# A two-layer hybrid decoder trunk on one core: four conditioning loads summed by TensorE behind the output projection, and slot weights read out of the transposed slot matrix

## The chip, the core and the metric

The kernel runs on one core of a Trainium2 chip. The metric is the device time of one execution in microseconds. Before the change it is 1552.6 us (median of 3 runs, 1552.41 to 1552.89).

## The reference, cut to what matters

256 tokens of width 1024 go through two layers in float32. Each layer has a token mixer (a combined input projection, three attention-like branches, per-channel gates, an output projection) and a mixture of experts. Both are conditioned: a vector `c` gives six rows of 1024 values per layer, two shifts, two scales and two gates of the residual.

```
c_act = silu(c)
for l in range(2):
    sh1, sc1, gt1, sh2, sc2, gt2 = split(c_act @ ada_w[l] + ada_b[l], 6)     # ada_w[l]: 1024 x 6144
    h = rms_norm(x, norm1_g[l]) * (1 + sc1) + sh1
    x = x + gt1 * token_mixer(h)                       # ends in merged @ out_w[l]
    h = rms_norm(x, norm2_g[l]) * (1 + sc2) + sh2
    group = argmax(softmax(h @ w_grp)); top 2 of the 8 experts in that group, weights w1, w2
    x = x + gt2 * sum over the token's two experts of weight * (silu(h @ W1[e]) * (h @ W3[e])) @ W2[e]
out = rms_norm(x, final_g)
```

There are 32 experts per layer; each has 6.3 MB of weights, so one layer of experts reads 201 MB from HBM.

## The kernel before, in words

**Loads.** All weights come over one queue (SP) in one order that is fixed when the program is built. A ring of slots of 1 MB receives them; the next load of the plan is issued as soon as its slot is given back, and SP issues strictly in order. The ring has 12 slots and grows for the expert stage: two tiles on the right side before the output projection, parts of the work area `ar`, and three tiles on the left side (`more_left`), which are the space of the split buffers that the mixer no longer needs. At most 8 loads are under way at a time.

**Conditioning ("ada").** `ada_w` is read in loads of 1 MB, 512 columns by half of the 1024 rows, 24 per layer. They are not needed at once, so they are spread behind the mixer's weights in the plan. A load is summed in one of two ways (`ada`, L485). By DVE: four instructions of 128x512 that add weight times `c` into `acc` (L509, L511), then one small matmul per 512 columns that adds up the partitions. Or by PE: four matmuls with the 32 columns of `cz` as stationary operand and the load as moving operand, each in a column strip of its own of the array. The loop `chain` (L1045) runs through the loads: twelve loads for this layer's second norm and first gate, all by DVE; then four loads for the second gate, and in layer 0 eight more for the next layer. It parks itself (`later`, L1039) before the last `ADA_TAIL` loads, and those go to PE: 2 in either layer, after the router's first part has been written.

**Output projection (`out`, L1167).** PE multiplies the merged branches with `out_w`, both split in a high and a low part, so three matmuls for each product. Column half n = 0 ends first, its residual (L588: DVE, DVE, then a square sum on ACT) and its half of the router (`router_half`, L1215: transposes of x, copies by ACT, products with the router's weights) run beside half n = 1. After half n = 1 the other half of the router follows. In ACT's queue the copy of the transposed first 128 tokens stands ahead of the square sum of the second 128.

**Routing (`route`, `choose`).** A chain of short DVE instructions, for the two token tiles alternately, finds group, experts and slots. For the first tile small matmuls without use (`pulse`) follow DVE's steps, to keep PE at work. At the end of the chain PE sums the slot counts (`mb`), DVE makes the first one-hot matrices, and PE gathers the tokens of the first pair of experts.

**Expert stage (`moe`, L1344).** 16 pairs of experts per layer, 64 slots for each expert. Per pair PE does: the first up projection (weights `exp_w1`), `combine` of the pair before (8 matmuls), `slots_of` (L1365), the second up projection (`exp_w3`), the gather of the next pair, four transposes, the down projection (`exp_w2`). `slots_of` makes unweighted one-hot matrices of tokens by slots, transposes them into PSUM, multiplies the untransposed ones with the weights W (two matmuls with 2 moving columns), copies each expert's 64 weights to `wsl` and the transposed matrix to `OT`. `wsl` scales the down projection's result of this pair; `OT` is used by `combine` one pair later.

Of the kernel before, what the change touches and what calls it, by code (L numbers as in the profile page):

```python
# [14 lines left out]
ALU = mybir.AluOpType  # L15
AX = mybir.AxisListType
# [4 lines left out]
NT = 2  # L21
# [3 lines left out]
CAP = 64  # L25
# [20 lines left out]
A_END = 9216  # L46


ADA_TAIL, ADA_FIRST = 2, 2

ADA_BEHIND = {2048: 1, 2560: 1, 0: 1}

# [113 lines left out]
class Trunk:  # L166
# [773 lines left out]
    def run(self, gen):  # L940
        for _ in gen:
            self.step(self.live)
# [84 lines left out]
    def mixer(self, l):  # L1027
        nc, run, finish = self.nc, self.run, self.finish
# [16 lines left out]
        def chain():  # L1045
            self.rowsA = yield from self.ada(l, 4, range(6), space, self.R, range(6))
            yield from self.gs(l, 1, 12 * l + 6, self.rowsA)
            yield from self.router_terms(l)
            while not self.y_free and gr not in self.live:
                yield  # L1050
            yield from self.gate_rows(12 * l + 4, A_GT1, self.rowsA)
            self.gated = True
            yield from later(0)
            self.rowsB = yield from self.ada(l, 10, range(2), lambda i: later(i + 1), self.v(A_RB, 512),
                                             range(min(2, inline // 2)))
            if l + 1 < DEPTH:
                rows = yield from self.ada(l + 1, 0, range(4), lambda i: later(i + 5 if i >= 0 else -1), self.acc[:, 1],
                                           range((inline - 4) // 2))
                yield from self.gs(l + 1, 0, 12 * l + 12, rows)
            self.parked = True  # L1060

        ga = chain()
# [104 lines left out]
        def out():  # L1167
            pa = [[self.bank("g") for _ in range(NT)] for _ in range(2)]
            for h in range(2):
                for n in range(2):  # L1170
                    for j in range(4):
                        wh, wl = self.next_w()
                        m = (self.yr[1], self.hr[0])[h][:, :, j]
                        for t in range(NT):
                            ts = slice(128 * t, 128 * t + 128)
                            self.mm3(pa[n][t], m[:, 0, ts], m[:, 1, ts], wh, wl, h + j == 0, h + j == 4)
                        self.pump()
                        yield
                    if h == 0:
                        continue  # L1180
                    if n:
                        self.finish(half)
                    half = self.router_half(n)
                    for t in range(NT):
                        self.residual(t, n, pa[n][t], self.v(A_RES + 512 * t, 512))
                        self.free(pa[n][t])
                        if n:
                            next(half)
                    if n:
                        self.together(half)  # L1190
                    else:
                        self.live.append(half)
# [6 lines left out]
        while not self.gated:  # L1199
            self.step(self.live)  # L1200
        run(out())
        while not self.parked:
            self.step(self.live)
        pool = self.open_extra(l, "left", 3)
        parts = [pool.tile([P, 2, 512], F32R, name=f"{n}_{l}", tag=n) for n in ("yh", "yl")]
        self.yp = [[p[:, n] for p in parts] for n in range(2)]
        self.ring.grow([self.v(A_MORE[2], 2048)], l)
        self.tail = True
        for _ in range(ADA_FIRST):
            next(ga, None)  # L1210
        self.route()
        self.rest = ga

# [33 lines left out]
    def choose(self, t, r):  # L1247
        nc = self.nc
        one = lambda: self.small(1)
        tt, tsc, red = nc.vector.tensor_tensor, nc.vector.tensor_scalar, nc.vector.tensor_reduce  # L1250
        stt = nc.vector.scalar_tensor_tensor
        rt = self.v(A_RT + 132 * t, 132)
        lg, lm, o1, o2 = rt[:, 0:36], rt[:, 36:68], rt[:, 68:100], rt[:, 100:132]
        stt(lg, self.psr[:, 64 * t:64 * t + 36], r, self.sb, ALU.mult, ALU.add)
        if t == NT - 1:
            self.free(self.psr)
        yield
        gmax, nmax, gsum, m2 = one(), one(), one(), one()
        g4 = lg[:, 0:4]
        c4, off = self.small(4), self.small(4)  # L1260
        red(gmax, g4, AX.X, ALU.max)
        yield
        stt(c4, g4, gmax, self.desc, ALU.is_equal, ALU.mult)
        self.pulse(t, c4)
        yield
        red(m2, c4, AX.X, ALU.max)
        self.pulse(t, m2)
        yield
        tsc(off, self.desc, m2, NEG, ALU.not_equal, ALU.mult)
        self.pulse(t, off)  # L1270
        yield
        tt(lm.rearrange("p (g e) -> p g e", g=4), lg[:, 4:36].rearrange("p (g e) -> p g e", g=4),
           off[:, :, None].to_broadcast([P, 4, 8]), ALU.add)
        yield
        top, idx, fi = self.small(8), self.small(8), self.small(2)
        nc.vector.max(top, lm)
        self.pulse(t, top)
        yield
        nc.vector.max_index(idx.bitcast(U32), top, lm)
        yield  # L1280
        nc.vector.tensor_copy(fi, idx[:, 0:2].bitcast(U32))
        yield
        tsc(o1, self.iota0, fi[:, 0:1], None, ALU.is_equal)
        self.pulse(t, o1)
        yield
        stt(self.mb[:, t], self.iota0, fi[:, 1:2], o1, ALU.is_equal, ALU.add)
        d, e2, den, w1, w2 = (one() for _ in range(5))
        ps = self.bank("s")
        if t == 1:
            self.mm(ps[:, 0:32], self.ones16, self.mb[:, 0], True, False)  # L1290
        self.mm(ps[:, 0:32], self.sU, self.mb[:, t], t == 0, True)
        yield
        tsc(nmax, gmax, -1.0, None, ALU.mult)
        tt(d, top[:, 1:2], top[:, 0:1], ALU.subtract)
        nc.scalar.activation(self.small(4), g4, AF.Exp, bias=nmax, accum_out=gsum)
        nc.scalar.activation(e2, d, AF.Exp)
        yield
        stt(self.rr[:, t], ps[:, 0:32], 1.0, self.mb[:, t], ALU.add, ALU.mult)
        self.free(ps)
        yield  # L1300
        self.one_hot(0, t, r)
        tsc(o2, self.iota0, fi[:, 1:2], None, ALU.is_equal)
        yield
        tsc(den, e2, 1.0, gsum, ALU.add, ALU.mult)
        yield
        nc.vector.reciprocal(w1, den)
        yield
        tt(w2, w1, e2, ALU.mult)
        tsc(self.W[:, t], o1, w1, None, ALU.mult)
        yield  # L1310
        stt(self.W[:, t], o2, w2, self.W[:, t], ALU.mult, ALU.add)
        yield

    def one_hot(self, p, t, by=None):

        oh = self.v(A_OH[t] + 2 * CAP * (p % 2), 2 * CAP)
        for i in range(2):
            e = 2 * p + i
            o, r = oh[:, CAP * i:CAP * i + CAP], self.rr[:, t, e:e + 1]
            if by is None:  # L1320
                self.nc.vector.tensor_scalar(o, self.iota1[:, 0:CAP], r, None, ALU.is_equal)
            else:
                self.nc.vector.tensor_scalar(o, self.iota1[:, 0:CAP], r, by, ALU.is_equal, ALU.mult)  # L1323
        return oh


# [17 lines left out]
    def moe(self, l):  # L1344
        nc, tc = self.nc, self.tc
# [4 lines left out]
        wsl = lambda p: self.wsl[:, p % 2:p % 2 + 1]  # L1350
# [9 lines left out]

        def wanted(p):

            return [self.one_hot(p, t, self.rs[:, t:t + 1]) for t in range(NT)]

        def slots_of(p):  # L1365

            ps = S[2]
            oh = [self.one_hot(p, t) for t in range(NT)]
            for t in range(NT):
                self.tr(ps[:, 128 * t:128 * t + 128], oh[t])  # L1370
            for t in range(NT):
                self.mm(ps[:, 256:258], oh[t], self.W[:, t, 2 * p:2 * p + 2], t == 0, t == 1)
            for e in range(2):
                es = slice(64 * e, 64 * e + 64)
                nc.vector.tensor_copy(wsl(p)[es], ps[es, 256 + e:257 + e])  # L1375
            nc.vector.tensor_copy(self.OT, ps[:, 0:256])

        def combine(p, halves=(0, 1)):

# [16 lines left out]
        for p in range(NE // 2):  # L1396
# [19 lines left out]
            elif p != OVERFLOW:  # L1416
                combine(p - 1)
            nc.scalar.activation(hid, G[0], AF.Silu)  # L1418
            slots_of(p)
            following = iter(()) if end else self.gather(wanted(p + 1), hg[(p + 1) % 2])  # L1420
            up(G[1], "exp_w3")
            nc.vector.tensor_tensor(hid, hid, G[1], ALU.mult)  # L1422
# [13 lines left out]
            ps = G[0]  # L1436
# [4 lines left out]
            for h, n0, nn in self.w2_parts(l, p):  # L1441
                sv = [self.ring.take((l, "exp_w2", 2 * p + e, h, n0)) for e in range(2)]
                for n in range(n0, n0 + nn):
                    for i in range(2):
                        j = 2 * h + i
                        for e in range(2):
                            es = slice(64 * e, 64 * e + 64)
# [193 lines left out]
```

## Time and profile before

| | |
|---|---|
| runs | 1552.6 us median (1552.41 to 1552.89) |
| profiled execution | 1548.41 us, of which the span is 1546.7 us |
| PE / PEld busy | 1471.0 / 901.9 us |
| DVE / ACT busy | 662.7 / 451.4 us |
| load queue (q1) | 532.89 MB, 85.3% of 16 DMA engines' span |
| granted TensorE clock, mean | 0.982 |

PE is TensorE's matmuls, PEld its weight loads, DVE VectorE, ACT ScalarE, SP the queue that issues the loads. [...] A float32 matmul shows as two records, a transpose as one. The two expert stages lie at 335 to 790 us and at 1081 to 1534 us; the two stretches from output projection to the first expert at 296 to 335 us and at 1044 to 1081 us.

### The profile page before, as it was taken

What the parts mean: (1) busy time and instruction counts of PE and PEld (TensorE: products, weight loads), DVE (VectorE), ACT (ScalarE), POOL (GpSimd) and SP (SyncE); (2) the same over time, 40 slices, a digit from 0 to 9 for tenths busy, and PEclk for the clock granted to TensorE, in tenths of its full rate; (3) what the DMA queues carried; (4) which work ended last, traced back from release to release, by engine and by line L of the source; (5) the groups of instructions that cost most, each with busy time, mean ns of one, the idle gap of its engine ahead of it and who ended that gap; (6) DMA issues with size and microseconds to landing.
All of it is one profiled execution on the core that took longest, in us unless ns stands there. A gap on an engine that the chain in (4) does not pass through costs nothing.

```text
span 1546.7 us, 21257 instructions
## 1 busy us (share of the span) xinstructions
PE 1471.0 (95%) x8326; PEld 901.9 (58%) x8326; DVE 662.7 (43%) x1756; ACT 451.4 (29%) x897; POOL 5.9 (0%) x10
## 2 busy tenths in 40 slices
PE   6898899999999999999979989999999999999996
PEld 3776889854444444444448779897444444444442
DVE  3766697951212222212157669767222222222223
ACT  3544544431111112111145554454211111111112
POOL 0000000000000000000000000000000000000001
PEclk9998999989999999999999999999999999999998
DMA  9963467989999999999995546667999999999993
GB/s 383 378 239 136 156 253 293 364 353 367 421 420 421 420 421 421 420 419 421 412 377 208 220 151 251 240 231 316 397 421 420 422 420 421 421 421 419 421 417 127
DMA packets 78542, 535.16 MB, mean 346 GB/s; under 512 B 8608, under 2 KB 8864, under 8 KB 15968
## 3 DMA queue, kind: packets, MB, share of 16 engines
q1 hardware_dynamic: 77776, 532.89, 85.3%
q8 instruction: 69, 1.13, 0.3%
q10 hardware_dynamic: 656, 0.80, 0.2%
q14 instruction: 41, 0.34, 0.1%
HBM read 532.61 MB, written 1.05 MB: 345 GB/s over the span
## 4 chain that ended last, share of the span: by engine, by line
PE 69%; DMA 15%; DVE 10%; ACT 4%; issue 2%; SPq 0%; DVEq 0%; ACTq 0%
PE bank L179 66%; DMA slot<-in_exp_w 6%; DMA more_left<-in_exp_w 3%; DVE ws L255 3%; DMA more_right<-in_exp_w 3%; PE bank L188 2%; DVE acc L511 2%; ACT ws L253 1%; DMA ar<-in_exp_w 1%; DMA slot<-in_w_in 1%; DMA slot<-in_ada_w 1%; ACT ar L664 1%; ACT ar L991 0%; ACT ar L1148 0%; DVE x L1392 0%
## 5 line engine op out<-in xcount | busy, mean ns | idle before, releaser
L179 PE MATMUL bank<-slot,ar 128*64 128x512 f32 (+1 forms) x1876 | 453.6, 593 | 1.0 <-ACT ar L1439 0.7
L179 PEld LDWEIGHTS bank<-slot,ar 128*64 128x64 f32 (+1 forms) x1876 | 143.0, 137 | 231.8 <-issue 214.7
L255 DVE TENSOR_TENSOR ws<-slot,ws 128x512 fp32r<-128x512 f32 (+1 forms) x276 | 187.5, 683 | 108.4 <-ACT ws L253 96.3
L179 PE MATMUL bank<-ar 128*64 128x512 f32 (+3 forms) x692 | 209.4, 502 | 4.3 <-DVE ar L887 3.1
L253 ACT CAST ws<-slot 128x512 fp32r<-128x512 f32 (+1 forms) x276 | 168.0, 618 | 141.1 <-PE bank L179 130.9
L179 PE MATMUL bank<-hr,ws 128*128 128x256 f32 x1536 | 202.4, 288 | 4.4 <-DVE ws L255 4.3
L179 PEld LDWEIGHTS bank<-hr,ws 128*128 128x128 f32 x1536 | 191.1, 193 | 13.5 <-DVE ws L255 5.4
L1341 ACT ACTIVATE ar<-bank,GS 128x128 f32<-128x128 f32 x128 | 58.6, 458 | 355.9 <-PE bank L179 325.2
L179 PE MATMUL bank<-ws,hr 128*128 128x512 f32 (+1 forms) x576 | 154.6, 415 | 7.2 <-ACT ws L253 3.4
L179 PE MATMUL bank<-more_left,ar 128*64 128x512 f32 x456 | 137.6, 594 | 0.0
L179 PEld LDWEIGHTS bank<-ar,x 128*128 128x128 f32 x1024 | 119.2, 192 | 25.1 <-issue 21.1
L179 PE MATMUL bank<-ar,x 128*128 128x128 f32 x1024 | 128.3, 278 | 1.8 <-DVE ar L1323 1.6
L179 PEld LDWEIGHTS bank<-ws,hr 128*128 128x128 f32 x576 | 109.4, 197 | 34.3 <-ACT ws L253 4.9
L179 PEld LDWEIGHTS bank<-ar 128*64 128x64 f32 (+2 forms) x692 | 81.4, 155 | 71.6 <-issue 59.3
L1458 DVE SCALAR_TENSOR_TENSOR yl<-bank,wsl,yh 128x512 fp32r<-128x512 f32 x60 | 45.0, 750 | 157.1 <-ACT yh L1457 157.1
L1375 DVE COPY wsl<-bank 64x1 f32<-64x1 f32 x64 | 10.0, 156 | 227.8 <-PE bank L179 227.4
L1339 DVE TENSOR_SCALAR ar<-bank,GS 128x128 f32<-128x128 f32 x128 | 52.4, 410 | 116.4 <-ACT ar L1341 116.4
L1422 DVE TENSOR_TENSOR R<-R,bank 128x512 f32<-128x512 f32 x32 | 22.0, 688 | 177.8 <-PE bank L179 177.8
L511 DVE SCALAR_TENSOR_TENSOR acc<-slot,cz,acc 128x512 f32<-128x512 f32 x122 | 90.8, 744 | 0.1
L179 PEld LDWEIGHTS bank<-more_left,ar 128*64 128x64 f32 x456 | 41.0, 137 | 82.5 <-issue 76.3
L1457 ACT ACTIVATE yh<-bank,wsl 128x512 fp32r<-128x512 f32 x60 | 41.2, 687 | 150.7 <-PE bank L179 150.7
L1418 ACT ACTIVATE R<-bank 128x512 f32<-128x512 f32 x32 | 19.2, 599 | 198.0 <-PE bank L179 198.0
(244 smaller groups left out, 1221.5 us busy)
## 6 DMA issues: line engine op xcount, KB each, us to landing
slot<-in_exp_w SPq DMA_DIRECT2D x226, 1024.0 KB, 19.8
ar<-in_exp_w SPq DMA_DIRECT2D x54, 1024.0 KB, 19.8
more_left<-in_exp_w SPq DMA_DIRECT2D x54, 1024.0 KB, 19.8
slot<-in_ada_w SPq DMA_DIRECT2D x46, 1024.0 KB, 6.8
more_right<-in_exp_w SPq DMA_DIRECT2D x38, 1024.0 KB, 19.3
slot<-in_w_in SPq DMA_DIRECT2D x24, 1024.0 KB, 10.4
slot<-in_gate_w SPq DMA_DIRECT2D x23, 1024.0 KB, 5.0
slot<-in_branch_w SPq DMA_DIRECT2D x12, 1024.0 KB, 4.8
```

Of the source, the lines that this page charges most:

```text
L179: self.nc.tensor.matmul(out, lhsT, rhs, start=start, stop=stop, skip_group_check=True)
L188: self.nc.tensor.transpose(out, in_, self.ident[:n, :n])
L253: self.nc.scalar.copy(hi, w)
L255: self.nc.vector.tensor_tensor(lo, w, hi.bitcast(F32), ALU.subtract)
L511: nc.vector.scalar_tensor_tensor(acc, v[:, t, :], c, acc, ALU.mult, ALU.add)
L664: nc.scalar.activation(s, s, AF.Exp, bias=nm[:, k:k + 1], accum_out=sm[:, k:k + 1])
L1339: nc.vector.tensor_scalar(hgT[:, j], pv[:, i], G[:, j:j + 1], S[:, j:j + 1], ALU.mult, ALU.add)
L1341: nc.scalar.activation(hgT[:, j], pv[:, i], AF.Identity, bias=S[:, j:j + 1], scale=G[:, j:j + 1])
L1418: nc.scalar.activation(hid, G[0], AF.Silu)
L1422: nc.vector.tensor_tensor(hid, hid, G[1], ALU.mult)
L1457: nc.scalar.mul(self.yp[n][0], G[n], wsl(p))
L1458: nc.vector.scalar_tensor_tensor(self.yp[n][1], G[n], wsl(p), self.yp[n][0].bitcast(F32), ALU.mult, ALU.subtract)
```

## The change

`ADA_TAIL` and `ADA_FIRST` go from 2 to 4. So the last four ada loads of each layer are planned behind the output projection's weights and go to PE; two of them were summed by DVE before. In layer 0 these two hold the next layer's third block of 512 columns, in layer 1 the first block of the second gate. In layer 1 `chain` now parks before any of the four. The sums of all four are issued inside `out`, when the matmuls of the last column half and the first half of the router have been written and before the last residual and the second half of the router. The three tiles of the left side join the ring after that. One of the useless matmuls (`pulse`) in `choose` goes. `slots_of` multiplies the weight into the one-hot matrix, transposes that, reads a slot's weight as the sum over the 256 tokens of its row, and `OT` as "not zero".

```diff
-ADA_TAIL, ADA_FIRST = 2, 2
+ADA_TAIL, ADA_FIRST = 4, 4
...
                     if n:
                         self.finish(half)
+                        while not self.parked:
+                            self.step(self.live)
+                        self.tail = True
+                        for _ in range(ADA_FIRST):
+                            next(ga, None)
                     half = self.router_half(n)
...
         run(out())
-        while not self.parked:
-            self.step(self.live)
         pool = self.open_extra(l, "left", 3)
...
         self.ring.grow([self.v(A_MORE[2], 2048)], l)
-        self.tail = True
-        for _ in range(ADA_FIRST):
-            next(ga, None)
         self.route()
...
         tsc(o1, self.iota0, fi[:, 0:1], None, ALU.is_equal)
-        self.pulse(t, o1)
...
-    def one_hot(self, p, t, by=None):
+    def one_hot(self, p, t, by):
...
-            if by is None:
-                self.nc.vector.tensor_scalar(o, self.iota1[:, 0:CAP], r, None, ALU.is_equal)
-            else:
-                self.nc.vector.tensor_scalar(o, self.iota1[:, 0:CAP], r, by, ALU.is_equal, ALU.mult)
+            self.nc.vector.tensor_scalar(o, self.iota1[:, 0:CAP], r, by(e), ALU.is_equal, ALU.mult)
...
             ps = S[2]
-            oh = [self.one_hot(p, t) for t in range(NT)]
             for t in range(NT):
-                self.tr(ps[:, 128 * t:128 * t + 128], oh[t])
-            for t in range(NT):
-                self.mm(ps[:, 256:258], oh[t], self.W[:, t, 2 * p:2 * p + 2], t == 0, t == 1)
-            for e in range(2):
-                es = slice(64 * e, 64 * e + 64)
-                nc.vector.tensor_copy(wsl(p)[es], ps[es, 256 + e:257 + e])
-            nc.vector.tensor_copy(self.OT, ps[:, 0:256])
+                self.tr(ps[:, 128 * t:128 * t + 128], self.one_hot(p, t, lambda e: self.W[:, t, e:e + 1]))
+            nc.vector.tensor_reduce(wsl(p), ps[:, 0:256], AX.X, ALU.add)
+            nc.vector.tensor_scalar(self.OT, ps[:, 0:256], 0.0, None, ALU.not_equal)
```

## Rows read from the trace of the kernel before

**Rows 1.** Busy time by stretch: window, PE, PEld, DVE, ACT, POOL, PEclk, DMA share, GB/s.
```profile
380.00:560.00 180.00, 180.00 (x954) 84.31 (x952) 38.95 (x113) 28.01 (x53) 0.00 (x0) 1.00 1.01 420
```
**Rows 2.** Chain that ended last, layer 0's expert stage: start us, us, what.
```profile
386.43 17.86 PE bank L179 x88
...
414.29 17.86 PE bank L179 x88
```
**Rows 3.** Waits of PE in 345 to 760 us: total, times, longest.
```profile
PE bank L179 <- DMA slot<-in_exp_w: 0.4, 1, 0.4
```
**Rows 4.** Two expert loads, late in layers 0 and 1: issue (timeline), time to landing.
```profile
738.95 0.33 SPq L139 DMA_DIRECT2D slot<-in_exp_w  x1
...
1480.88 0.33 SPq L139 DMA_DIRECT2D slot<-in_exp_w  x1
...
DMA to landing us min/median/max: 19.8/19.8/19.8
```
**Rows 5.** Timeline of PE where these loads are used: start us, us, what.
```profile
761.11 4.46 PE L179 MATMUL bank<-slot,ar 128*64 128x512 f32 x19
765.50 0.50 PE L179 MATMUL bank<-yh,OT 128*128 128x512 f32 x1
...
1508.92 0.50 PE L179 MATMUL bank<-yh,OT 128*128 128x512 f32 x1
```
**Rows 6.** Timeline of PE in slots_of of layer 1's last pair.
```profile
1511.12 0.51 PE L179 MATMUL bank<-rt,ar 128*128 128x2 f32 x4
1511.55 0.65 PE L179 MATMUL bank<-slot,ar 128*64 128x512 f32 x2
```
**Rows 7.** Groups by line and shape, DVE: count, busy us, mean ns, idle before.
```profile
L663 DVE TENSOR_REDUCE sm<-ar 128x1 f32<-128x256 f32 x16 | 6.5, 408 | 0.0
```
**Rows 8.** Timeline of layer 0, projection to first gather.
```profile
313.30 3.90 DVE L511 SCALAR_TENSOR_TENSOR acc<-slot,cz,acc 128x512 f32<-128x512 f32 x5
...
314.68 0.60 PE L188 MATMUL bank<-cst,x 128*128 128x128 f32 x4
...
319.31 1.95 PE L188 MATMUL bank<-cst,x 128*128 128x128 f32 x8
...
324.82 0.42 DVE L1254 SCALAR_TENSOR_TENSOR ar<-bank,rs,sb 128x36 f32<-128x36 f32 x2 [1.02 <-PE bank L179]
...
330.04 0.29 DVE L1298 SCALAR_TENSOR_TENSOR rt<-bank,mb 128x32 f32<-128x32 f32 x2 [2.02 <-PE bank L179]
...
330.85 4.21 PE L179 MATMUL bank<-ar,x 128*128 128x128 f32 x32 [0.80 <-DVE ar L1323]
```
**Rows 9.** Timeline of layer 1, projection to first gather.
```profile
1067.63 1.92 PE L179 MATMUL bank<-cst,ar 128*128 128x36 f32 x16
...
1069.38 1.07 PE L188 MATMUL bank<-cst,x 128*128 128x128 f32 x8
...
1072.80 1.93 PE L179 MATMUL bank<-slot,cz 128*32 128x512 f32 x16
...
1073.33 0.42 DVE L1254 SCALAR_TENSOR_TENSOR ar<-bank,rs,sb 128x36 f32<-128x36 f32 x2
...
1074.54 1.04 PE L179 MATMUL bank<-cst,sm 128*4 128x128 f32 x8
...
1076.45 0.28 DVE L1298 SCALAR_TENSOR_TENSOR rt<-bank,mb 128x32 f32<-128x32 f32 x2
```
**Rows 10.** Busy time by stretch, columns as in Rows 1, around routing and layer 1's projection.
```profile
319.00:329.20 10.20, 10.20 (x49) 6.80 (x49) 7.09 (x50) 3.25 (x8) 0.00 (x0) 0.50 1.01 426
...
1063.00:1077.00 14.00, 12.96 (x94) 9.49 (x92) 10.90 (x59) 5.52 (x14) 0.00 (x0) 1.00 0.73 288
...
1000.00:1014.00 14.00, 14.00 (x115) 13.39 (x113) 12.66 (x21) 7.63 (x14) 0.00 (x0) 1.00 0.67 243
```
**Rows 11.** Timeline of PE, layer 1: partition sum of two DVE-summed loads.
```profile
1013.39 1.04 PE L179 MATMUL bank<-acc,cz 128*32 128x512 f32 x2
1014.37 0.86 PE L179 MATMUL bank<-hr,ws 128*128 128x256 f32 x5
```

More of the change, by code (lines that the diff above doesn't have):

```diff
@@ L1300, in choose @@
         yield
-        self.one_hot(0, t, r)
+        self.one_hot(0, t, lambda e: r)
         tsc(o2, self.iota0, fi[:, 1:2], None, ALU.is_equal)
@@ L1361, in wanted @@
         def wanted(p):
-            return [self.one_hot(p, t, self.rs[:, t:t + 1]) for t in range(NT)]
+            return [self.one_hot(p, t, lambda e: self.rs[:, t:t + 1]) for t in range(NT)]
         def slots_of(p):
             ps = S[2]
-            oh = [self.one_hot(p, t) for t in range(NT)]
             for t in range(NT):
-                self.tr(ps[:, 128 * t:128 * t + 128], oh[t])
-            for t in range(NT):
-                self.mm(ps[:, 256:258], oh[t], self.W[:, t, 2 * p:2 * p + 2], t == 0, t == 1)
-            for e in range(2):
-                es = slice(64 * e, 64 * e + 64)
-                nc.vector.tensor_copy(wsl(p)[es], ps[es, 256 + e:257 + e])
-            nc.vector.tensor_copy(self.OT, ps[:, 0:256])
+                self.tr(ps[:, 128 * t:128 * t + 128], self.one_hot(p, t, lambda e: self.W[:, t, e:e + 1]))
+            nc.vector.tensor_reduce(wsl(p), ps[:, 0:256], AX.X, ALU.add)
+            nc.vector.tensor_scalar(self.OT, ps[:, 0:256], 0.0, None, ALU.not_equal)
         def combine(p, halves=(0, 1)):
```

## The prediction

> **What bounds the kernel now.** I read the stretches first, then the chain of waits, PE's waits, and last the timelines where the change sits. In the expert stage PE is busy all the time, 180.00 of 180 us, and so is the load queue, at 420 GB/s [rows 1]. Both look like the bound. The chain goes through PE, and one pair of experts comes every 414.29 - 386.43 = 27.86 us [rows 2]. A pair's weights are 12 loads of 1.049 MB; at 420 GB/s a load takes 2.50 us, a pair 30.0 us. So the queue is slower than PE, and PE lives on what the ring held when the stage began. PE waited for a load 0.4 us in 415 us [rows 3], so that stock lasts. How far it lasts decides what a faster PE can gain. In the last pair of layer 0 the load issued at 738.95 landed 19.8 us later, at 758.8 [rows 4]. Its 16 matmul records are the last of the 19 that run from 761.11 to 765.50 [rows 5]; 16/19 of 4.39 us is 3.7 us, so it is used from 761.8: 3.0 us to spare. In layer 1: landing 1480.88 + 19.8 = 1500.7, use 1508.92 - 3.7 = 1505.2: 4.5 us to spare. **PE sets the end of both stages, but the queue is only 3.0 and 4.5 us behind it.**
>
> **Slots' weights (slots_of).** Removed per pair are two matmuls with 2 columns, 4 records. They stand between the transposes and the next projection; from their start to the next projection's is 1511.55 - 1511.12 = 0.43 us [rows 6]. The trace bounds the gain by 0 and by their busy time, 0.51 us; I take 0.43, since PE works without a gap there. For 16 pairs that is 6.9 us of PE per layer. On DVE two copies go and a reduction of 128x256 comes, 0.41 us by the one in softmax [rows 7]; that one reads SBUF and this one PSUM; I take 0.41, and nothing and twice that as its bounds. The cover is DVE's own idleness, 180 - 39 us of 180 [rows 1]: `wsl` is wanted only by the down projection's result and `OT` one pair later. If the cover were gone, it would cost 0.8 us a pair. The one-hot matrices that the transposes wait for gain a second operation, and they are written while PE runs the first up projection. Nothing there.
>
> PE cannot cash the 6.9 us. From the last pairs on it is bound by landings, so of each stage's end only the spare time is gained, plus whatever the queue itself gains or loses at its restart, plus the last pair's own 0.43.
>
> **Conditioning, layer 0.** Removed from DVE are two loads' sums, eight instructions. Five of them (313.30, 3.90 us) stand in DVE's queue ahead of the last residual, which so begins at 317.2, although PE is ready for it [rows 8]. Added on PE are two more loads, and all four now stand behind the router's first half. Two loads take 1074.54 - 1072.80 = 1.74 us at full clock [rows 9], so four take 3.5. New order on PE: transposes of the first half at 314.68 [rows 8], 0.54 us for the four of them (half of 1.07), products with the router's weights for 1069.38 - 1067.63 = 1.75 us [rows 9], then the four loads, 3.5. The second half's transposes start at 320.5 instead of 319.31 [rows 8]: 1.2 later. The residual is ready by then. From here the path runs at full clock, as in layer 1: 1073.33 - 1069.38 = 3.95 us to the first step of the choice, and 1076.45 - 1073.33 = 3.12 to the slot counts [rows 9]; in layer 0 before, these took 5.5 and 5.2, because the clock was at 0.50 (1.2 GHz) from 319.0 to 329.2 [rows 10], after PE had waited for DVE's sums, and because the two ada loads and the useless matmuls lay in front of the counts (2.02 us of waiting for PE) [rows 8]. So the counts come at 320.5 + 7.1 = 327.6 instead of 330.04: 2.4 us earlier, up to 3.2 if the two other DVE sums that go (0.75 each) also held up the residual of half n = 0. Against this stands the clock: with the ada matmuls gone from the choice, PE has only `pulse` in it, and the gather (4.21 us) [rows 8] may run at 1.2 GHz and take 4.2 us more. Between -1.3 (2.9 - 4.2) and 3.2 earlier I take the middle, 0.8: layer 1's choice kept 1.00 on a shorter pause [rows 10], layer 0's did not. The load queue there waits for slots that PE gives back, so its restart moves by that, and by 0.43 from the first pair.
>
> Sum for layer 0: the stage's end moves by 3.0 (spare) + 0.8 + 0.43 (restart) + 0.43 (last pair) = **4.7 us** earlier, and all of layer 1 with it.
>
> **Conditioning, layer 1.** The eight DVE sums that go lie at 1000 to 1014, beside a PE that is busy 14.00 of 14 us [rows 10]; nothing is gained by them except the partition sum on PE, 1014.37 - 1013.39 = 1.0 us [rows 11] less one matmul's spacing of 0.1: 0.9. At the projection's end there is no DVE queue to be cleared: PE goes from the router's first half (1067.63) straight to the transposes at 1069.38 [rows 9]. The four loads come between, and everything behind waits 3.5 us: transposes, ACT's copy, behind it ACT's square sum of the second tile, and DVE's chain that needs it. The two loads that they replace ran in the shadow of that chain (1072.80 to 1074.54, next to 1073.33) and cost nothing. Then the clock: 0 to 4.2 us for the gather, 2.1 taken. And the queue: two loads that came early before now hold slots until PE is through, so two loads more, 2 x 2.50 = 5.0 us, are behind the restart, and SP, in order, issues the three `more_left` loads only behind these slots. The queue's idleness in 1063 to 1077, 14 x (1 - 288/420) = 4.4 us [rows 10], could hide all but 0.6 of that. I take 4.2 later, near the upper end, because the idleness lies ahead of the slots' release, which PE now sets.
>
> At the last pair: PE would be 3.5 + 2.1 - 15 x 0.43 = 0.9 us earlier, the landings are 4.2 later than before with 4.5 to spare, so 0.3 earlier; the later of the two decides: 0.3. With 0.9 and the last pair's 0.43: **1.6 us** earlier.
>
> **Other edits.** The `pulse` that goes costs PE 0.2 to 0.4 us beside DVE's work; nothing. The weights of gate, branch and projection come two loads earlier, where nothing waits for them; nothing. The four ada loads stand ahead of the first expert load in the queue and have landed long before.
>
> **Sum.** 4.7 + 1.6 = 6.3 us. Against the profiled span of 1546.7 that is 1540.4; the profiled execution took 1548.4, 4.2 less than the median of the runs, so I take the difference from the median: 1552.6 - 6.3 = **1546.3 us**. With both ends of every bound: at best 3.0 + 3.2 + 0.86 in layer 0 and in layer 1 0.9 + 2.95 (PE: 3.5 - 6.45) + 0.43, 11.4 in all; at worst 3.0 - 1.3 + 0.86 in layer 0, and in layer 1 landings 5.0 + 4.2 later: +4.7 - 0.9 - 0.43, so 0.8 slower. This case's own range is 1541.2 to 1553.4.
>
> **Rivals.**
> *The clock.* The choice becomes a pause on PE, and both gathers run at 1.2 GHz. For it: the low stretch of layer 0 [rows 10]; against it: layer 1 went through its choice at 1.00. Price: layer 0 gains 2.6 instead of 4.7; in layer 1 half of 4.2 us reaches the queue, landings 6.3 later, +1.8 - 0.9 - 0.43 = 0.5 slower. Together 2.1 faster: 1550.5. [...]
> *The queue.* The stages' ends follow the load queue already, in the runs if not in the profiled execution, which was 4.2 us faster than they: then there is no spare time to gain. Layer 0 gains 0.8 + 0.43 = 1.2, layer 1 loses 4.2 - 0.9 = 3.3: 2.1 slower, 1554.7. For it: 420 GB/s throughout [rows 1]; against it: 0.4 us of waiting [rows 3].
> *The pairs get no shorter* (the slower side). If the new weighted one-hot or the reduction holds PE up by as much as the two matmuls gave, at `slots_of`, PE keeps 27.86 us a pair: layer 0 gains 0.8, layer 1 loses 3.5 + 2.1 - 0.9 = 4.7: 3.9 slower, 1556.5. It decides as long as less than 3.9 / 32 = 0.12 us is gained for each of the 32 pairs. Against it: DVE's idleness [rows 1].
> *The sums wait for their loads*, so the change does not do what it says: each load that lands late costs up to 2.50 us on PE behind the projection, at most 10 us for a layer's four: 1556.3 with one layer's. Against it: loads are issued long ahead in order.
>
> **How the numbers follow.** Forecast 0.52, clock 0.15, queue 0.18, pairs 0.11, loads 0.04. A measurement of this kernel tells about 0.2%, 3.1 us, from no change. Faster by more: 0.50 of the forecast, 0.05 of the clock, 0.02 of the others, 0.57. Slower by more: 0.08 of the pairs, 0.05 of the queue, 0.02 of the loads, 0.15. The rest, 0.28, is no change. The range runs from 1541.5 over the queue's time to 1554.7.
>
> **What would show it.** Right: pairs of 27.4 us early in the stage; spare time of landings near zero in the last pair of either layer, and waits of PE for loads there; layer 0's gather near 330, layer 1's 3.5 us or more later against the projection's end; PE's sums of four loads between router products and transposes. Wrong: pairs still at 27.86; waits for loads from the middle of the stage on; PE low in the first projections; layer 1's landings not later.

## The result and the profile after

| | runs | profiled execution | mean granted clock |
|---|---|---|---|
| before | 1550.7 us median (1544.8 to 1552.9, 6 runs) | 1548.41 us, span 1546.7 | 0.982 |
| after | 1557.9 us median (1554.1 to 1561.8, 6 runs) | 1555.81 us, span 1554.2 | 0.976 |

The ratio is 1.0051 with an interval of 1.0032 to 1.0069: slower by 0.5%, where 6.3 us faster was forecast. Executions of one kernel differ by up to 9 us (28 of the kernel before, timed later, took 1544.9 to 1554.3), so medians of several are compared.

The pairs of experts did get shorter. Timeline of PE in the changed kernel, the same loads one pair apart (start us, us, what): 413.32 - 385.79 = 27.53 us, where [rows 2] gave 27.86.

```profile
385.79 2.75 PE L179 MATMUL bank<-slot,ar 128*64 128x512 f32 x12
...
413.32 2.75 PE L179 MATMUL bank<-slot,ar 128*64 128x512 f32 x12
```

Layer 0's experts started 2.8 us earlier (332.15 below; 335.0 before), and at the last loads of pair 11 PE was 6.7 us ahead of the kernel before (663.5 and 670.2). When pair 12 began, 0.9 us of that was left. Timeline of PE at the overflow check ahead of pair 12 in layer 0, after:

```profile
669.36 0.40 PE L179 MATMUL bank<-yl,OT 128*128 128x512 f32 x1
675.91 3.68 PE L179 MATMUL bank<-more_right,ar 128*64 128x512 f32 x8 [6.16 <-PEq L1476]
```

and before:

```profile
676.02 0.40 PE L179 MATMUL bank<-yl,OT 128*128 128x512 f32 x1
676.81 2.76 PE L179 MATMUL bank<-more_right,ar 128*64 128x512 f32 x11 [0.39 <-DMA slot<-in_exp_w]
```

L1476 (L1485 before) is `with tc.If(flag > 0)` in `overflow`: each engine compares a flag and, where no expert has more than 64 tokens, jumps over a loop that would serve the surplus. PEldq is the instruction queue of PE, ACTq, DVEq and SPq are those of the others. By source line, after (count, ns min/median/max, first and last start):

```profile
L1476 ACTq COMPARE_BRANCH  x2: 45/50/54, 667.8 to 1417.2; - x2
...
L1476 DVEq COMPARE_BRANCH  x2: 63/68/72, 668.6 to 1418.0; - x2
...
L1476 PEldq COMPARE_BRANCH  x2: 6105/6156/6208, 669.4 to 1418.8; - x2
...
L1476 SPq COMPARE_BRANCH  x2: 45/48/50, 686.9 to 1435.6; - x2
```

and before:

```profile
L1485 PEldq COMPARE_BRANCH  x2: 445/454/462, 676.1 to 1418.4; - x2
```

PE's jump takes 6.2 and 6.1 us instead of 0.45, in both layers. No other engine is late: ACT and DVE had jumped before, and SP comes to its own jump 11 us after PE has gone on. The waits of PE name it rightly in layer 0 and wrongly in layer 1: it names a load into `ar`, but the matmul reads a slot, whose load had landed at 1408.7, 16.5 us before (us in total, times, longest; one row of each stage):

```profile
PE bank L179 <- PEq L1476: 6.2, 1, 6.2
...
PE bank L179 <- DMA ar<-in_exp_w: 5.9, 1, 5.9
```

The one "wait for a load" of [rows 3], 0.4 us, is the same thing: it ends at 676.81 in the lines above, and PE's branch before lasts from 676.05 to 676.50. The load that the matmul there reads had landed at 662.8.

In the pause PE's granted clock drops to 0.50, and it stays low behind it. Busy time by stretch, after (columns as in [rows 1]): the branch in layer 0, layer 1's routing, the branch in layer 1.

```profile
671.70:681.90 10.20, 5.99 (x14) 1.91 (x16) 0.98 (x4) 0.00 (x0) 0.00 (x0) 0.50 1.02 417
1077.90:1084.70 6.80, 5.39 (x26) 5.08 (x26) 4.23 (x29) 2.71 (x9) 0.00 (x0) 0.50 1.02 425
1422.60:1429.50 6.90, 4.31 (x12) 1.40 (x14) 0.98 (x4) 0.00 (x0) 0.00 (x0) 0.51 1.01 417
```

In the first of these stretches the 14 records of 512 columns take 5.99 us, 0.43 each, or 1.2 columns a ns; the 16 of the load at 663.53, at a clock of 1.00, take 3.54 us (to 667.07), 0.22 each, or 2.3. The profile gives the clock as a share alone: the prediction's 1.2 GHz is the 0.50 of its rows. At 0.50 for most of it, the first load of pair 12 takes 6.5 us in layer 0 (675.91 to 682.36) and 5.6 in layer 1 (1425.19 to 1430.76), instead of 3.5. So the branches cost 5.7 + 3.0 and 5.6 + 2.1 us more than before, 16.4 in all.

Routing in layer 0, timeline of PE and one step of DVE after, to be held against [rows 8]:

```profile
313.12 1.92 PE L179 MATMUL bank<-cst,ar 128*128 128x36 f32 x16
314.97 1.93 PE L179 MATMUL bank<-slot,cz 128*32 128x512 f32 x16
...
317.57 1.04 PE L179 MATMUL bank<-slot,cz 128*32 128x512 f32 x8
318.54 1.09 PE L188 MATMUL bank<-cst,x 128*128 128x128 f32 x8
...
325.63 0.29 DVE L1297 SCALAR_TENSOR_TENSOR rt<-bank,mb 128x32 f32<-128x32 f32 x2
...
326.43 5.79 PE L179 MATMUL bank<-ar,x 128*128 128x128 f32 x32 [0.75 <-DVE ar L1319]
332.15 5.37 PE L179 MATMUL bank<-slot,ar 128*64 128x512 f32 x24
```

and in layer 1, against [rows 9]:

```profile
1066.35 1.92 PE L179 MATMUL bank<-cst,ar 128*128 128x36 f32 x16
1068.20 1.92 PE L179 MATMUL bank<-ar,cz 128*32 128x512 f32 x16
1069.94 1.90 PE L179 MATMUL bank<-slot,cz 128*32 128x512 f32 x16
1071.77 1.09 PE L188 MATMUL bank<-cst,x 128*128 128x128 f32 x8
...
1079.66 6.32 PE L179 MATMUL bank<-ar,x 128*128 128x128 f32 x32 [0.75 <-DVE ar L1319]
1085.91 2.37 PE L179 MATMUL bank<-slot,ar 128*64 128x512 f32 x10
```

### The profile page after: what moved, and what is told of

It reads as the page before. It is cut to its first block, busy times and chain, and to the rows that moved or that the text cites. A ratio compares the mean times of both kernels' runs of the same rounds, so it can differ in the third digit from the quotient of the medians.

```text
span 1554.2 us, 20994 instructions
## 1 busy us (share of the span) xinstructions
PE 1464.7 (94%) x8222; PEld 888.9 (57%) x8222; DVE 661.8 (43%) x1708; ACT 451.2 (29%) x897; POOL 5.9 (0%) x10
## 4 chain that ended last, share of the span: by engine, by line
PE 45%; DVE 6%; DMA 3%; ACT 2%; issue 1%; DVEq 0%; ACTq 0%; SPq 0%
PE bank L179 44%; DVE ws L255 1%; PE bank L188 1%; DMA slot<-in_exp_w 1%; DMA ar<-in_exp_w 1%; DVE acc L511 1%; ACT ws L253 1%; DVE x L1383 0%; DVE R L1382 0%; ACT ar L664 0%; DMA slot<-in_ada_w 0%; ACT ar L991 0%; DVE sm L210 0%; DVE ar L669 0%; DVE ar L852 0%
## 5 line engine op out<-in xcount | busy, mean ns | idle before, releaser
L179 PE MATMUL bank<-slot,ar 128*64 128x512 f32 (+1 forms) x1888 | 458.9, 596 | 6.6 <-DMA ar<-in_exp_w 5.9
L255 DVE TENSOR_TENSOR ws<-slot,ws 128x512 fp32r<-128x512 f32 (+1 forms) x284 | 193.2, 684 | 120.5 <-ACT ws L253 110.6
L253 ACT CAST ws<-slot 128x512 fp32r<-128x512 f32 (+1 forms) x284 | 172.9, 618 | 144.0 <-PE bank L179 130.4
L179 PEld LDWEIGHTS bank<-ar,x 128*128 128x128 f32 x1024 | 123.3, 197 | 24.8 <-issue 21.1
L179 PE MATMUL bank<-ar,x 128*128 128x128 f32 x1024 | 132.2, 284 | 1.5 <-DVE ar L1319 1.5
L179 PE MATMUL bank<-more_left,ar 128*64 128x512 f32 x448 | 131.3, 597 | 0.0
L1366 DVE TENSOR_REDUCE wsl<-bank 128x1 f32<-128x256 f32 x32 | 13.6, 425 | 214.1 <-PE bank L188 214.1
L179 PE MATMUL bank<-more_right,ar 128*64 128x512 f32 x312 | 75.5, 628 | 6.2 <-PEq L1476 6.2
```

The lines of the kernel that those rows point to most:

```text
L179: self.nc.tensor.matmul(out, lhsT, rhs, start=start, stop=stop, skip_group_check=True)
L253: self.nc.scalar.copy(hi, w)
L255: self.nc.vector.tensor_tensor(lo, w, hi.bitcast(F32), ALU.subtract)
L1366: nc.vector.tensor_reduce(wsl(p), ps[:, 0:256], AX.X, ALU.add)
```

## The experiments

Two theories for the branch. **F (fetch):** what the jump costs depends on where it and its target stand in PE's list of instructions; the change took some 200 of 17,662 instructions out and moved it. **Q (queue):** PE, now early, waits at the branch for what SP has yet to issue; SP does issue a load at 675.74 and at 1424.66, within 0.6 us of PE's restart in either layer. The trace speaks against Q by SP's late branch, but only moving the branch alone can decide. Places are counted in the built program. In the kernel before the branch is PE's instruction 7371 in layer 0 and 16083 in layer 1, in the changed one 7299 and 15908; the jump passes 444 instructions in both.

**The branch put back in its place.** After, with matmuls without use (2 instructions each):

```diff
             for l in range(DEPTH):
+                for _ in range((36, 52)[l]):
+                    self.mm(self.S[2][:, 0:32], self.ident[:, 0:64].bitcast(BF16), self.ident[:, 0:16].bitcast(BF16), True, True)
                 self.mixer(l)
```

> The changed kernel with 36 small matmuls without use before the mixer of layer 0 and 52 before that of layer 1 (in PE's pauses, 2 instructions each), so that the branch of the overflow check stands where it stands in the kernel before: PE instruction 7371 and 16084 instead of 7299 and 15908. Theory F (PE's taken branch over the 444 instructions of the overflow loop costs 6.1 us or 0.45 us by where it stands in PE's instruction stream): the branch falls from 6.2 and 6.1 us to 0.45 in both layers, PE stays at full clock behind it, and the time is 1541 to 1545 us, as forecast or a little better. Theory Q (PE, arriving earlier, waits there for what SP has yet to issue): the branch keeps 6 us, the time stays at 1557.9 or a little above.

Measured: 1541.9 us (1539.1 to 1545.3) beside 1549.3 for the kernel before; ratio 0.9947 (0.9929 to 0.9964). The branch:

```profile
L1476 PEldq COMPARE_BRANCH  x2: 458/460/462, 673.5 to 1414.7; - x2
```

88 matmuls without use make the changed kernel 16 us faster. Q is refuted.

**The kernel before, its branch moved.** The same lines in the kernel before with (50, 0).

> The kernel before with 50 small matmuls without use before the mixer of layer 0, which move the branch of the overflow check by 100 PE instructions in both layers (7371 to 7471, 16083 to 16183) and change nothing else. Theory F, if 256 instructions are a block and only a target in the next block is cheap: both branches rise from 0.45 to about 6.1 us, PE's clock falls behind them, and the time rises by 2 x (5.7 + 2 to 3), to 1564 to 1568 us. Theory Q: branches stay at 0.45 us, the time within 2 us of the kernel before, 1550.7.

Measured: 1570.7 us (1564.8 to 1570.8), ratio 1.0118 (1.0091 to 1.0144).

```profile
L1485 PEldq COMPARE_BRANCH  x2: 6068/6074/6080, 675.5 to 1432.2; - x2
```

The cost is not the change's: the kernel before has it too, once its branch is moved by 100 instructions. Branches and the low clock behind them (5.9 and 6.5 us for the first loads of pair 12) make 16.6 of the 21.4 us. The rest, by which the time is above the expected 1564 to 1568 us, lies in layer 1's mixer, in another low stretch, whose cause was not tested. Two of the six executions took only 1564.8 and 1565.6 us, at a mean clock of 0.975 and 0.976 where the other four had 0.972 to 0.973. The stretch in the profiled one, of 1570.8 us:

```profile
994.00:1007.70 13.70, 13.70 (x64) 13.46 (x65) 5.97 (x14) 1.82 (x3) 0.00 (x0) 0.50 0.71 273
```

**A shorter jump.** The overflow loop's two passes become an inner loop; the jump passes 268 instructions. In the changed kernel and in the one before:

```diff
-                for b in range(2):
+                for t in range(NT):
+                    nc.vector.tensor_scalar(col[:, 4 + t:5 + t], col[:, t:t + 1], float(CAP), None, ALU.subtract)
+                with tc.For_i(0, 2, 1) as b:
                     for t in range(NT):
-                        nc.vector.tensor_scalar(col[:, 4 + t:5 + t], col[:, t:t + 1], float(CAP + P * b), None, ALU.subtract)
...
+                    for t in range(NT):
+                        nc.vector.tensor_scalar(col[:, 4 + t:5 + t], col[:, 4 + t:5 + t], float(P), None, ALU.subtract)
```

> The changed kernel with the two passes of the overflow loop's body written as an inner loop, so that the branch skips 268 PE instructions and not 444. Theory F: a target so near lies one block ahead, 0.45 us in both layers, 1541 to 1545 us. Theory Q: 6 us as before, 1557.9 us.

> The kernel before with the same inner loop. Both theories: branches of 0.45 us or less, 1550.7 us within 2. If the shorter loop itself gained something, it would show here.

Measured: after 1543.7 us (1539.4 to 1548.3), ratio 0.9960 (0.9943 to 0.9978); before 1549.4 us, ratio 1.0003 (0.9986 to 1.0020). Branches, after and before:

```profile
L1476 PEldq COMPARE_BRANCH  x2: 323/338/352, 669.3 to 1412.5; - x2
```

```profile
L1485 PEldq COMPARE_BRANCH  x2: 445/446/447, 675.9 to 1418.7; - x2
```

So with a cheap branch the change gains 5.7 us, and the loop itself nothing. (The branch made cheap by its place gave 1549.3 to 1541.9, 7.3; the two intervals overlap.) The changed kernel is 14.2 us faster for the loop and 16.0 for the place, where the branches cost 16.4; these differences are within the spread. In this version the last pair of layer 0 meets its load, as forecast. Timeline of PE (the load was issued at 734.28 and landed 21.2 us later, at 755.5; against [rows 4, 5]):

```profile
750.69 4.50 PE L179 MATMUL bank<-slot,ar 128*64 128x512 f32 x18
755.55 3.65 PE L179 MATMUL bank<-slot,ar 128*64 128x512 f32 x14 [0.35 <-DMA slot<-in_exp_w]
```

**The parts of the change, branch cheap.** All with the inner loop: only `slots_of` and the one-hot; only the four loads behind the projection; the whole change with the `pulse` put back; the same with four loads in layer 0 alone. Edits of the last two, against the changed kernel:

```diff
         tsc(o1, self.iota0, fi[:, 0:1], None, ALU.is_equal)
+        self.pulse(t, o1)
```

```diff
-ADA_TAIL, ADA_FIRST = 4, 4
+ADA_TAIL = (4, 2)
...
-                    if n:
+                    if n and l == 0:
                         while not self.parked:
...
         self.ring.grow([self.v(A_MORE[2], 2048)], l)
+        if l:
+            self.tail = True
+            for _ in range(2):
+                next(ga, None)
         self.route()
```

> The kernel before with the inner loop in the overflow path (branch over 268 PE instructions) and, of the change, only the new slots_of and the weighted one-hot. Theory S (the prediction's terms hold once the branch is cheap): 27.5 us per pair; layer 0 ends 3.4 to 4 us earlier, when its last pair waits for landings; layer 1 gains its spare 5 us too: 8 to 9 us, 1540 to 1542 us, so better than the whole change. Theory N (the pairs bring nothing beyond layer 0's spare time, the gain comes from conditioning): 1545 to 1547 us.

> The kernel before with the inner loop and, of the change, only ADA_TAIL = ADA_FIRST = 4 with the sums behind the projection (slots_of and the useless matmul as before). Theory S: layer 0's experts start 1 to 3 us earlier, which PE keeps; layer 1's start about 4.5 us later against layer 0's end, its landings as well; together 2 to 4 us slower than before with the inner loop, 1551 to 1553 us. Theory N: 1546 us, faster.

> The changed kernel with the inner loop and the useless matmul that the change took out of choose put back. If that matmul keeps PE's clock up through routing: the gathers run at 1.00 in both layers, layer 1's experts start up to 2 us earlier, 1541 to 1542 us. If it does nothing: 1543.7 us within 1.5, the low stretch at the gather (0.50 for 6.8 us) as in the changed kernel.

> The changed kernel with the inner loop and the useless matmul, and four loads behind the projection in layer 0 alone; layer 1 sums two by DVE and two by PE at the place before. Theory S: layer 1's experts and its landings come about 4.6 us earlier than with four, 1538 to 1540 us, the best of all. Theory N: layer 1's place costs nothing, 1542 to 1544 us.

| version, all with the cheap branch | us, median | ratio to before | interval |
|---|---|---|---|
| `slots_of` alone | 1539.5 | 0.9935 | 0.9911 to 0.9959 |
| four loads alone | 1553.1 | 1.0027 | 1.0012 to 1.0043 |
| whole change, `pulse` back | 1542.9 | 0.9956 | 0.9941 to 0.9972 |
| whole change, `pulse` back, four loads in layer 0 alone | 1538.9 | 0.9931 | 0.9906 to 0.9956 |

Theory S held in all (`slots_of` alone came out 0.5 us under its range): `slots_of` alone gains some 9 us and the conditioning loses 4, about all of it in layer 1: with its loads left at the old place 4.0 us come back. The useless matmul does nothing that can be measured. The last version is the fastest; `slots_of` alone can't be told from it.

**How far is too far.** The changed kernel with 444 instructions to jump, and the branch at two other places: (21, 50) and (55, 50) useless matmuls.

> The changed kernel (branch over 444 instructions) with 21 small matmuls before layer 0's mixer and 50 before layer 1's, which put the branches at PE instructions 7341 and 16050, 173 and 178 in blocks of 256. Known so far, place in a block: slow at 131, 47 (layer 0), 36, 55 (layer 1); cheap at 203 (layer 0), 211 and 212 (layer 1). If the branch is cheap just when its target lies in the next block of 256, the cheap places are a window 512 - 444 = 68 wide, and of 173 here and 241 in the run beside it exactly one is cheap in layer 0, and of 178 and 246 exactly one in layer 1. If the block is not 256, or the place is not what decides, both or neither can be.

> The same with 55 and 50 small matmuls: branches at 7409 and 16118, 241 and 246 in blocks of 256. With the window of 68: cheap (0.45 us) in a layer in which the run beside it is slow (6.1 us), and slow where that is cheap; with two layers on different sides, one slow branch in each run and some 1549 us in both.

Measured: 1556.9 and 1545.3 us (one execution each, 1548.6 before). In the first both branches are slow, in the second both cheap, one of two in each layer as the window asks:

```profile
L1476 PEldq COMPARE_BRANCH  x2: 6128/6239/6350, 668.6 to 1419.3; - x2
```

```profile
L1476 PEldq COMPARE_BRANCH  x2: 445/454/462, 669.9 to 1412.4; - x2
```

In the second PE has to wait even so: it stops some 30 instructions later, with nothing that the profile could name ("issue"), until 676.17: 6.3 us after the branch began at 669.91. Timeline of PE:

```profile
670.67 3.19 PE L179 MATMUL bank<-more_right,ar 128*64 128x512 f32 x13 [0.39 <-PEq L1476]
676.17 0.65 PE L179 MATMUL bank<-more_right,ar 128*64 128x512 f32 x2 [2.31 <-issue]
```

By place modulo 256 (what is left of the place after whole blocks), a jump over 444 was cheap at 203, 211, 212, 241 and 246 and slow at 36, 47, 55, 131, 173 and 178; the twelve jumps over 268 were all cheap. So the cheap places lie within 44 neighbouring ones with none of the slow ones among them, and a window of 68 holds them, as expected. That a cheap jump's target lies in the next block was not shown: no trace says where a block begins.

The traces also hold packets on a queue for instructions. The page of the kernel before lists it, and windows of 0.2 us find single packets: after, at 672.9 to 673.1, and in the run with the branch at 241, at 673.6 to 673.8 (queue, packets, MB, share):

```profile
q8 instruction: 69, 1.13, 0.3%
...
q8 instruction: 1, 0.02, 36.8%
...
q8 instruction: 1, 0.02, 34.3%
```

69 packets of 16.4 KB for 17,662 instructions of PE are 256 to a packet, an estimate that counts every packet of this queue as PE's. In both layers of the kernels before and after a packet starts 3.5 to 3.7 us after PE's branch (at 679.69 and 1422.12 before, at 672.98 and 1422.28 after) and takes 1.0 to 1.2 us. Behind the cheap jump in layer 0 before PE works meanwhile, from 676.81 on. At the slow one after it stands still from the branch at 669.39 on; the packet starts at 672.98, and PE goes on at 675.91. That PE waits for this packet is inferred from the order; what it holds no trace shows.

The branch takes 6.1 to 6.4 us where it stalls. Whether that would be shorter beside an idle load queue stays open: in the stretches read the queue was at 413 to 417 GB/s, and of the 6 us the packet itself is 1.2 in either layer after.

## Why the prediction was wrong

Forecast 1546.3 us, range to 1554.7; measured 1557.9. With the branch made cheap in both kernels the change takes 1549.4 to 1543.7 us, 5.7 faster, where the sum said 6.3. So the sum was nearly right for what it held, in part because its errors below have opposite signs, and **a term was missing from it**.

- **The step that failed** is the path through the expert stage: "one pair of experts comes every 414.29 - 386.43 = 27.86 us" was carried through to the last pair, so the jump between pair 11 and pair 12 was a term put at no change, without a reason. The sum took that stretch as it was, and [rows 3] as a wait for a load. In its place the runs showed a jump whose cost hangs on PE's count of instructions: 2 x 5.7 us and 2.1 to 3.0 us of low clock behind each. In "Other edits", too, instructions taken from PE were priced by their busy time alone.
- **`slots_of`:** 0.43 us a pair was forecast, 0.33 measured. Without the two matmuls the next projection starts 0.36 us after the transposes (685.91 to 686.27), where 0.27 us after them the two had begun (683.83 to 684.10): 0.1 of the 0.43 stayed. The reduction took 425 ns (estimate 410) and hid as said; by shape, after: count, busy us, mean ns.

```profile
L1366 DVE TENSOR_REDUCE wsl<-bank 128x1 f32<-128x256 f32 x32 | 13.6, 425 | 214.1 <-PE bank L188 214.1
```

- **The spare time of 3.0 and 4.5 us:** used up, once the branch is cheap. In that run PE waits for a load in layer 0's last pair (755.55 above), and uses its last loads 2.6 us after landing, not 6.0; layer 1's second loads of the last pair land as PE wants them. From its `combine` to that of the pair before, the last pair takes 759.13 - 730.18 = 28.95 us in layer 0 and 1502.19 - 1474.54 = 27.65 in layer 1, where the pair before takes 27.52: landings cost 1.4 and 0.1 us. So "PE cannot cash the 6.9 us" held in layer 0; in layer 1 PE's pace and the landings meet within 0.1 us, and with `slots_of` alone PE cashes there all that it saves (27.52 for the last pair too).
- **Conditioning, layer 0:** the counts came 4.4 us earlier (325.63; 330.04 in [rows 8]), not 2.4. 1.4 of that stood already at the transposes of column half n = 0 (309.24; 310.61 before), ahead of the new order; its cause is open. 0.6 came up to the next transposes (312.69; 314.68 before), where PE before had also waited 0.23 us for DVE's part of `ws`. The 2.4 behind them are those of the forecast. The gather took 5.79 instead of 4.21 us at a clock that was low for part of it (0.50 in 323.6 to 330.3): 1.6 lost. From the first of these transposes to the first expert it is 22.9 us instead of 24.4. So the new order gained 1.5, and the forecast was 0.8. All four traces with the old order have 24.4, all eight with the new one 22.9 to 23.4. (The 0.8 was to be the middle of -1.3 and 3.2, which is 0.95.)
- **Conditioning, layer 1:** four loads take 1071.77 - 1068.20 = 3.57 us (3.5 forecast). The clock took 2.1 us from the gather (6.32 and 4.21), the middle of 0 to 4.2 that was chosen; nothing in the rows had pointed to the middle, so that is luck. Landings, counted from layer 0's end, come 4.9 later with the cheap branch (4.2 forecast). Leaving two loads at the old place gave 4.0 us back, so the part of the forecast that spoke against the change was real.
- **Rivals.** "The pairs get no shorter" named 1556.5, near the result, by luck: its mechanism is refuted, 27.53 us a pair. "The queue" fell: without the branch there was spare time to gain. The clock's price in routing was met in part (1.6 and 2.1 us), and the loads were there when PE summed them. What happened was none of them.

## What to carry to other kernels

Here edits that added or removed instructions ahead of PE's branch changed its cost, though they touched nothing there: find every `If` and loop in the profile by its source line, read the engine's own branch row, and price it at either value (here 0.45 or 6.1 us, and the clock behind it). Keep what a usually false `If` jumps over short; here 268 instructions instead of 444 made every branch cheap, 0.32 to 0.46 us. (These are twelve branches; whether a jump over 268 is cheap at every place was not shown.) And read small waits with care: 0.4 us put down to a load that had landed 14 us before was the only trace of it.

## What was not expected of the hardware

- PE's taken jump over 444 instructions cost 0.45 to 0.46 us or 6.07 to 6.35 us, by place alone, and one over 268 cost 0.32 to 0.46 us; ACT's and DVE's took 0.05 to 0.07 us throughout, over code of their own.
- In the four pauses of 6 us behind a branch in the changed kernel and in the one before with its branch moved, PE's granted clock fell to 0.50 before PE went on, and it stayed there for 6.8 to 10.2 us in all. In the kernel before, with 0.3 to 0.4 us of pause there, it stayed at 1.00.
- Matmuls without use that only move a branch made the changed kernel 1% faster, 1541.9 us instead of 1557.9.
- Each of these taken jumps of PE in the kernels before and after, cheap or slow, was followed 3.5 to 3.7 us later by a packet of 16.4 KB on the instruction queue.
